# Moving the weights and activations to other places in their 256-byte period, and another order of matmuls in the first layer

## The chip, the cores and the metric

The kernel runs on one core of one Trainium2 chip. The metric is device microseconds of one execution. Before the change it takes 2504.57 us (median of 3 runs, 2503.95 to 2505.67).

## The reference

A two-layer encoder on 272 tokens (16 meta tokens and 256 tokens of input), width 2048, everything in float32. One layer is:

```
h = RMSNorm(x)
[q | k | v | f | ga | gf] = h @ W_in
a = attention(q, k, v) @ W_attn_br ; s = Re(2-D DFT of f) @ W_four
x = x + (sigmoid(ga) * a + sigmoid(gf) * s) @ W_out
x = x + W_down( silu(dwconv3(RMSNorm(x) @ W_up_gate)) * (RMSNorm(x) @ W_up_val) )
```

The meta tokens are dropped at the end. Nearly all the work is products of the activations (272 tokens wide) with weight matrices that are each read once.

## The kernel before

**Three matmuls for one product.** Activations and weights are float32. TensorE runs them in a format of shorter mantissa, so each operand is cut into a high part (a rounded copy) and a low part (what is left), and a product is made of three matmuls: high weights with high activations, high weights with low activations, low weights with high activations. Below they are called a *triple*. In the code they are lines 384, 385 and 386 in `group`, in that order. The weights are the stationary operand (a 128x128 load ahead of each matmul), the activations the moving one: 272 columns in the first layer, and in the second 258 (columns 14 to 271) but for the keys and values, which have 272.

**Chunks and groups.** Weights come in chunks of 512 rows by 256 columns: CW = 4 row blocks (`c`) by MG = 2 column blocks (`m`) of 128x128. `load_raw` (L266) brings a chunk from memory through SP's DMA queue, `split_w` makes the high part on ScalarE (L313) and the low part on VectorE (L315), four row blocks in one instruction each, two chunks ahead of the chunk in use (LOOK = 2). `group` runs all chunks of one pair of output blocks: `ps[0]` and `ps[1]` are two accumulators in PSUM, and a chunk has 4 x 2 = 8 triples, 24 matmuls. In all chunks but a group's last the order is c = 0, m = 0; c = 0, m = 1; c = 1, m = 0 and so on, so that two triples in a row read the same activations. In a group's last chunk it is c = 0 to 3 for m = 0, and then c = 0 to 3 for m = 1, so that the first accumulator is done half a chunk early. This is the sort at L370 and L371. After each second triple `step()` and `pump()` hand out other work (norms, rotary, splits), whatever the order.

**Which groups there are.** The first layer has groups of 4 chunks (f 2 and 3, k, v, four q, eight ga, eight gf, 22 ug, 22 uv), of 2 chunks (eight a, sixteen o), of 6 (eight d) and of 5 (eight d): 108 groups, 408 chunks, of which 300 are not the last of their group. Two more f groups are run by `first_groups`, which has an order of its own, and the s groups by `four_group`. In the second layer `group` runs k, v, q, ga, gf, a, o and ug, 224 chunks, and the uv groups that are left (L380, L381); the rest of that layer, `ps_p` and `ps_t`, has the activations stationary and 512 columns of weights moving (L1474, L1555).

**Where the operands lie.** A row of activations is 272 x 4 = 1088 bytes, 4 x 256 + 64. A row block of a chunk is given the same 1088 bytes (CS = T), of which 1024 are used. So when `c` goes up by one, activations and weights both move by 64 bytes within a period of 256 bytes, and their distance within that period stays what it was. The distance is set by where tiles begin: the constants X_AT, G_AT, M_AT and Q_AT are numbers of float32 by which the activations are moved into their tiles (xHL; gHL; mH and mL; qH and qL), and W_PAD puts 128 bytes between the three buffers of high weights and those of low weights. LOW = 60 puts the low activations of a tile at 16 bytes less than the high ones within the period. Worked out from the sizes of the tiles in the order in which they are allocated, in bytes modulo 256, at c = 0 and the first column that a matmul uses:

| | high activations | low activations | high weights | low weights |
|---|---|---|---|---|
| before, both layers | 108 | 92 | 128 | 0 |
| before, keys and values of layer 2 | 52 | 36 | 128 | 0 |
| before, split activations of `ps_p` (`opnd`, stationary) | 128 | 128 | 128 | 0 |

The order of the instructions on TensorE is that of the program. There is no wait in `group` other than those for the split weights, for the activations and for a free PSUM bank.

Of the kernel before, what the change touches and what calls it, by code (L numbers as in the profile page):

```python
# [10 lines left out]
F32 = mybir.dt.float32  # L11
F32R = mybir.dt.float32r
# [4 lines left out]
P = 128  # L17
# [15 lines left out]
CW = 4  # L33
# [28 lines left out]
F0 = 1536  # L62
CS = T
LOW = 60
X_PAD, X_AT = 192, (59, 45)
G_AT, G_PAD = 43, 128
M_AT, M_PAD = ((27, 23), (5, 1)), (60, 22)
Q_AT, Q_PAD = (((43,), (47,)), ((45, 29), (41, 41))), (((76,), (84,)), ((62, 46), (62, 62)))
W_PAD = 32
A_PAD, O_AT = 48, 16  # L70

def _branch(text):
# [91 lines left out]
def encoder_kernel(ctx, tc, xT, params, consts, bmat, cfold, csign, w_fl, w_f64c, w_in, w_abr, w_four, w_f64, w_out, w_up, w_down, w_vn, w_dn, w_dt, out):  # L164
    nc = tc.nc
    per = ctx.enter_context(tc.tile_pool(name="per", bufs=1))
    wp = ctx.enter_context(tc.tile_pool(name="wp", bufs=3))
# [10 lines left out]
    for l in range(DEPTH):  # L178
        def g(w, mg, k0, k1):
            return [(w[l, mg, c], CW) for c in range(k0 // CW, k1 // CW)]  # L180
# [11 lines left out]
        for half in range(2):  # L192
            for kind, j in BRANCH_ORDER[half]:
                w, off, n = {"ga": (w_in, IN_GA, KT), "gf": (w_in, IN_GF, KT), "s": (w_four, 0, 8), "a": (w_abr, 0, 8)}[kind]
                chs = [(fw[KT + 2 * j + c], CW) for c in range(2)] if (l, kind) == (1, "s") else g(w, off + j, 0, n)
# [23 lines left out]
    chunks, folded, streamed, mix, summed, stage, small_w = [], set(), set(), {}, {}, {}, {}  # L219
    t, done = 0, 0  # L220
# [25 lines left out]
    raws, splits = {}, {}  # L246
# [24 lines left out]
    def advance(upto):  # L271
        while st["raw"] < min(upto + RAW + extra(upto), len(chunks)):
            load_raw(st["raw"])
            st["raw"] += 1
        while st["fetch"] < min(upto, len(chunks)):
            i = st["fetch"]
            if i in folded:
                todo.append((i, lambda i=i: fold_w(i)))
            for a in (0, 2) if i <= 3 else (0,):
                todo.append((i, lambda i=i, a=a: split_w(i, a, a + 2 if i <= 3 else CW)))  # L280
            st["fetch"] += 1

    def pump(upto=None):
        if upto is None:
            if todo:
                todo.pop(0)[1]()
        while upto is not None and todo and todo[0][0] <= upto:
            todo.pop(0)[1]()
# [7 lines left out]
    def weight_rows(w, dense):  # L296
        if dense:
            return w[:, :CW * MG * P].rearrange("p (c m) -> p c m", c=CW)
        return w.rearrange("p (c m) -> p c m", c=CW)[:, :, :MG * P]

    def split_w(i, a, b, parts="hl"):
        if i not in splits:
            new = []
            for t in ("wh", "wl"):
                new.append(weight_rows(wp.tile([P, CW * CS], F32R, tag=t, name=f"{t}{i}"), i in streamed))
                if i == 0:
                    wp.tile([P, W_PAD], F32, tag=t + "_pad", name=t + "_pad", bufs=1)
            splits[i] = tuple(new)
        h, lo = splits[i]
        st["wl"] = lo  # L310
        r = raws[i]
        if "h" in parts:
            nc.scalar.copy(h[:, a:b], r[:, a:b])  # L313
        if "l" in parts:
            nc.vector.tensor_tensor(lo[:, a:b], r[:, a:b], h[:, a:b].bitcast(F32), op=ALU.subtract)  # L315
            if b == CW:
                del raws[i]
# [8 lines left out]
    def step(force=False):  # L326
        if not force and slow[1] and slow[2]:
            slow[0] -= 1
            if slow[0] <= 0:
                slow[0] = slow[2]  # L330
                if next(slow[1], None) is None:
                    slow[1] = None
        for s in shadow:
            s[0] -= 1
        for s in list(shadow):
            if force or s[0] <= 0:
                try:
                    s[0] = next(s[1])
                except StopIteration:
                    shadow.remove(s)  # L340
                return
# [9 lines left out]
    def next_split():  # L351
        i = st["next"]
        advance(i + 1 + LOOK)
        pump(i)
        st["next"] += 1
        return splits.pop(i)

    def group(key, rhs, width, tag="mm"):
        k, chs = order[st["grp"]]
        assert k == key, (k, key)  # L360
        st["grp"] += 1
        nm = "_".join(str(v) for v in key)
        ps = [psum.tile([P, 512], F32, tag=tag, name=f"ps_{nm}_{m}") for m in range(MG)]
        nk = CW * len(chs)
        for j in range(len(chs)):
            for _ in range(mix.get((key, j), 0)):
                next(st["products"])
            h, lo = next_split()
            cm = [(c, m) for c in range(CW) for m in range(MG)]
            if j == len(chs) - 1:  # L370
                cm.sort(key=lambda v: v[1])  # L371
            for n, (c, m) in enumerate(cm):
                kt = CW * j + c
                x = rhs(kt)
                sl = slice(m * P, (m + 1) * P)
                o = ps[m][:, :width]
                if len(x) == 1:
                    ab = x[0]
                    o2 = ps[m][:, :2 * width].rearrange("p (r n) -> p r n", r=2)
                    nc.tensor.matmul(o2, h[:, c, sl], ab, start=kt == 0, stop=False)  # L380
                    nc.tensor.matmul(o, lo[:, c, sl], ab[:, 0, :], start=False, stop=kt == nk - 1)  # L381
                else:
                    a, b = x
                    nc.tensor.matmul(o, h[:, c, sl], a, start=kt == 0, stop=False)  # L384
                    nc.tensor.matmul(o, h[:, c, sl], b, start=False, stop=False)  # L385
                    nc.tensor.matmul(o, lo[:, c, sl], a, start=False, stop=kt == nk - 1)  # L386
                if n % 2:
                    step()
                    pump()
        return ps  # L390
# [36 lines left out]
    def first_groups(pss):  # L427
# [4 lines left out]
        for kt in range(KT // CW * 2 * CW):  # L432
            q, j, c = kt // (2 * CW), kt // CW % 2, kt % CW
            k = CW * q + c
            if c == 0:
                if kt == 0:
                    norm_split(0, P_NM)
                    split_w(0, 0, 1)
                    norm_split(1, P_NM)
                    split_w(0, 1, 2)  # L440
                    norm_split(2, P_NM)
                    split_w(0, 2, 4)
                    norm_split(3, P_NM)
                    st["fetch"] = 1
                h, lo = splits.pop(st["next"])
                st["next"] += 1
# [194 lines left out]
    for l in range(DEPTH):  # L641
# [7 lines left out]
        with tc.tile_pool(name=f"mix{l}", bufs=1) as mp:  # L649
# [105 lines left out]
            if l == 0:  # L755
# [19 lines left out]
                with tc.manual_schedule(engines={mybir.EngineType.PE, mybir.EngineType.DVE}):  # L775
                    ps = group((l, "f", 2), xr(0), T, "aux")
# [7 lines left out]
                tc.keep_in_program_order(nc.vector.tensor_tensor(br3[64:96], brem[32:64], br3[32:64].bitcast(F32), op=ALU.subtract))  # L784
                tc.keep_in_program_order(nc.vector.tensor_scalar(bgh, prm[:, P_BG:P_BG + DEPTH * 2 * KT], 0.5, None, op0=ALU.mult))
                f_evac(3, group((l, "f", 3), xr(0), T))
            else:
                push(norm_stats(hold), 8)
# [188 lines left out]
            VL = mp.tile([P, NKV, 2, P], F32R, name="VL")  # L977

            ps = group((l, "k", 0), xr(0), T)
            until(hold, "tok2")  # L980
            tok, tok2 = hold["tok"], hold["tok2"]
# [220 lines left out]
            for i in range(4):  # L1202
# [3 lines left out]
                if last:  # L1206
                    if i in (0, 2):
                        until(hold, "vt" if i == 0 else "fold")
                        for t_, n in ((qH, "q1"), (qL, "q2")):
                            o = Q_AT[l][t_ is qL][i // 2]  # L1210
                            t = mp.tile([P, 4 * T + Q_PAD[l][t_ is qL][i // 2]], F32R, tag=n + "ab"[i // 2], name=n)
                            t_.append(t[:, o:o + 4 * T].rearrange("p (h t) -> p h t", t=T))
                elif i == 0:
                    until(hold, "vt")
                    until(hold, "fold")
                    for t_, n in ((qH, "q1"), (qL, "q2")):
                        o = Q_AT[l][t_ is qL][0]
                        t = mp.tile([P, NH * T + Q_PAD[l][t_ is qL][0]], F32R, tag=n, name=n)[:, o:o + NH * T].rearrange("p (h t) -> p h t", t=T)
# [26 lines left out]
            for half in range(2):  # L1245
                mH = mL = None
                for n_, (kind, i) in enumerate(BRANCH_ORDER[half]):
                    if half or last and n_ >= 4:
                        slow[2] = 22
                    j = i - 4 * half  # L1250
# [42 lines left out]
        with tc.tile_pool(name=f"ffn{l}", bufs=1) as fp:  # L1293
# [32 lines left out]
            for c, n in enumerate(() if last else FF_SPLIT):  # L1326
                gf = fp.tile([P, FF_SPLIT[0] * 2 * T + G_PAD], F32R, tag="gHL", name="gHL")
                gH, gL = (gf[:, G_AT + (FF_SPLIT[0] * T + LOW) * r:G_AT + (FF_SPLIT[0] * T + LOW) * r + FF_SPLIT[0] * T].rearrange("p (k t) -> p k t", t=T) for r in range(2))
                for i in range(k0 // MG, (k0 + n) // MG):
                    cs = conv_gate(i)  # L1330
                    ps = group((l, "uv", i), xr(0), T)
                    for m in range(MG):
                        j = 2 * i + m - k0
# [10 lines left out]
            if last:  # L1344
# [152 lines left out]
                for i in UP_ORDER:  # L1497
# [16 lines left out]
                    for m in range(0 if i in VPAIRS else MG):  # L1514
                        j = 2 * i + m
# [21 lines left out]
                for b in TAIL_ORDER:  # L1537
                    k, chs = order[st["grp"]]
# [5 lines left out]
                    for j in range(len(chs)):  # L1544
                        for _ in range(mix.get((k, j), 0)):
                            next(st["products"])
                        wh, wl = (w.rearrange("p (k a) m -> p k (a m)", k=2) for w in next_split())
# [86 lines left out]
```

## Time and profile before

| | |
|---|---|
| median of the runs | 2504.57 us |
| the profiled execution's own time | 2504.27 us |
| its span, first to last instruction | 2502.3 us |
| TensorE busy | 2493.7 us (100%), 18848 matmuls |
| weight loads busy | 2411.3 us (96%) |
| VectorE, ScalarE, GpSimd busy | 1987.5, 1338.4, 204.8 us |
| DMA | 706.85 MB, 282 GB/s |

Matmuls are pipelined, and the ends that the profile gives are modelled: a matmul of 272 columns is shown with some 283 ns, while the next one starts some 123 ns after it. So what a stretch of matmuls costs is read from starts: the start of the first matmul of the next stretch less that of its own first.

### The profile page before, as it was taken

How to read it: one execution, taken by the hardware profiler on the slowest of the kernel's cores; microseconds unless marked ns; L12 is line 12 of the kernel's file. 1: busy time of each engine (PE TensorE's matmuls, PEld its weight loads, DVE VectorE, ACT ScalarE, POOL GpSimd, SP SyncE). 2: the span in 40 equal slices, each digit the busy share in tenths (PEclk: the TensorE clock that was granted, in tenths of full speed). 3: DMA queues.
4: the chain of work that ended last, by engine and by line, in shares of the span. 5: the costliest groups of instructions: out<-in, count | busy, mean ns of one | idle time of the engine just before them, and what ended most of it. 6: DMA issues, size and time to landing. Idle time of an engine off the chain costs nothing.

```text
span 2502.3 us, 47930 instructions
## 1 busy us (share of the span) xinstructions
PE 2493.7 (100%) x18848; PEld 2411.3 (96%) x18848; DVE 1987.5 (79%) x3155; ACT 1338.4 (53%) x1913; POOL 204.8 (8%) x394
## 2 busy tenths in 40 slices
PE   9999999999999999999999999999999999999999
PEld 9999999999999999999999999999988899988887
DVE  7787866778878667888778887666878787898898
ACT  6455534454444334444445565444676665666665
POOL 0000000012212222222210000000000000000000
PEclk9999999999999999999999999999999999999999
DMA  7544557879989999999985647888878886788887
GB/s 250 170 156 163 189 195 250 261 259 373 400 323 381 402 389 373 397 380 391 391 294 199 197 151 246 267 262 273 252 268 293 296 291 237 260 282 293 283 298 267
DMA packets 194802, 706.85 MB, mean 282 GB/s; under 512 B 22144, under 2 KB 27392, under 8 KB 194320
## 3 DMA queue, kind: packets, MB, share of 16 engines
q1 hardware_dynamic: 146768, 517.09, 58.1%
q0 software_dynamic: 46368, 184.57, 21.3%
q8 instruction: 147, 2.41, 0.4%
q10 hardware_dynamic: 1440, 2.13, 0.2%
q14 instruction: 79, 0.65, 0.1%
HBM read 623.32 MB, written 111.15 MB: 294 GB/s over the span
## 4 chain that ended last, share of the span: by engine, by line
PE 100%; DMA 0%; DVE 0%; ACT 0%; SPq 0%; issue 0%
PE ps_p L1474 14%; PE ps_ug L386 7%; PE ps_ug L384 7%; PE ps_ug L385 7%; PE ps_d L386 3%; PE ps_uv L386 3%; PE ps_uv L384 3%; PE ps_d L384 3%; PE ps_uv L385 3%; PE ps_d L385 3%; PE ps_o L385 2%; PE ps_ga L385 2%; PE ps_ga L386 2%; PE ps_gf L384 2%; PE ps_gf L385 2%; PE ps_ga L384 2%
## 5 line engine op out<-in xcount | busy, mean ns | idle before, releaser
L315 DVE TENSOR_TENSOR wl<-raw,wh 128x1024 fp32r<-128x1024 f32 (+1 forms) x961 | 1158.7, 1217 | 397.8 <-ACT wh L313 388.2
L313 ACT CAST wh<-raw 128x1024 fp32r<-128x1024 f32 (+1 forms) x961 | 996.8, 1042 | 888.1 <-PE ps_ug L385 201.7
L384 PE MATMUL ps_ug<-xHL,wh 128*128 128x272 f32 (+1 forms) x1408 | 398.6, 283 | 0.0
L386 PE MATMUL ps_ug<-xHL,wl 128*128 128x272 f32 (+1 forms) x1408 | 397.0, 283 | 0.0
L385 PE MATMUL ps_ug<-xHL,wh 128*128 128x272 f32 (+1 forms) x1408 | 396.8, 282 | 0.0
L385 PEld LDWEIGHTS ps_ug<-xHL,wh 128*128 128x128 f32 x1408 | 265.5, 189 | 3.3
L384 PEld LDWEIGHTS ps_ug<-xHL,wh 128*128 128x128 f32 x1408 | 263.9, 187 | 3.6
L386 PEld LDWEIGHTS ps_ug<-xHL,wl 128*128 128x128 f32 x1408 | 263.4, 188 | 0.9 <-DVE wl L315 0.4
L1474 PE MATMUL ps_p<-wh,opnd 128*128 128x512 f32 x816 | 222.9, 393 | 0.0
L384 PE MATMUL ps_uv<-xHL,wh 128*128 128x272 f32 x704 | 201.1, 286 | 0.0
L384 PE MATMUL ps_d<-gHL,wh 128*128 128x272 f32 x704 | 201.1, 286 | 0.0
L386 PE MATMUL ps_d<-gHL,wl 128*128 128x272 f32 x704 | 201.0, 285 | 0.0
L386 PE MATMUL ps_uv<-xHL,wl 128*128 128x272 f32 x704 | 200.9, 285 | 0.0
L385 PE MATMUL ps_uv<-xHL,wh 128*128 128x272 f32 x704 | 199.8, 284 | 0.0
L385 PE MATMUL ps_d<-gHL,wh 128*128 128x272 f32 x704 | 199.7, 284 | 0.0
L1474 PEld LDWEIGHTS ps_p<-wh,opnd 128*128 128x128 f32 x816 | 148.3, 188 | 29.7 <-ACT wh L313 0.2
L547 DVE TENSOR_TENSOR wi<-wi,wi 128x512 f32<-128x512 f32 x224 | 147.0, 684 | 0.1
L384 PE MATMUL ps_ga<-xHL,wh 128*128 128x272 f32 (+1 forms) x512 | 146.7, 287 | 0.0
L384 PE MATMUL ps_gf<-xHL,wh 128*128 128x272 f32 (+1 forms) x512 | 145.7, 285 | 0.0
L385 PE MATMUL ps_o<-mL,wh 128*128 128x272 f32 (+1 forms) x512 | 144.8, 283 | 0.0
L384 PE MATMUL ps_o<-mH,wh 128*128 128x272 f32 (+1 forms) x512 | 144.6, 282 | 0.0
L386 PE MATMUL ps_ga<-xHL,wl 128*128 128x272 f32 (+1 forms) x512 | 144.6, 282 | 0.0
(381 smaller groups left out, 5952.4 us busy)
## 6 DMA issues: line engine op xcount, KB each, us to landing
raw<-in_w_up SPq DMA_DIRECT2D x288, 512.0 KB, 6.3
raw<-in_w_in SPq DMA_DIRECT2D x191, 512.0 KB, 4.0
raw<-in_w_down SPq DMA_DIRECT2D x88, 512.0 KB, 7.0
wi<-in_w_dn POOLq DMA_DIRECT2D x80, 512.0 KB, 9.2
ft<-wi POOLq DMA_DIRECT2D x80, 512.0 KB, 7.3
raw<-ft SPq DMA_DIRECT2D x80, 512.0 KB, 4.7
raw<-in_w_out SPq DMA_DIRECT2D x64, 512.0 KB, 4.3
raw<-fv SPq DMA_DIRECT2D x64, 512.0 KB, 4.5
```

Of the source, the lines that this page charges most:

```text
L313: nc.scalar.copy(h[:, a:b], r[:, a:b])
L315: nc.vector.tensor_tensor(lo[:, a:b], r[:, a:b], h[:, a:b].bitcast(F32), op=ALU.subtract)
L384: nc.tensor.matmul(o, h[:, c, sl], a, start=kt == 0, stop=False)
L385: nc.tensor.matmul(o, h[:, c, sl], b, start=False, stop=False)
L386: nc.tensor.matmul(o, lo[:, c, sl], a, start=False, stop=kt == nk - 1)
L547: tt = lambda *v, **kw: tc.keep_in_program_order(nc.vector.tensor_tensor(*v, **kw))
L1474: nc.tensor.matmul(ps[h], x, w[:, 512 * h:512 * h + 512], start=fresh and (s_, q) in BEGIN and first, stop=(s_, q) in END and end, skip_gr ...
```

## The change

The weights' padding goes, so that high and low weights both begin at 128 within the period, and all the activations are moved by 64 bytes up (X_AT of the first layer by 48 float32 down, which is the same within the period):

| | high activations | low activations | high weights | low weights |
|---|---|---|---|---|
| after, both layers | 172 | 156 | 128 | 128 |
| after, keys and values of layer 2 | 116 | 100 | 128 | 128 |
| after, `opnd` | 128 | 128 | 128 | 128 |

If the period is cut into four lines of 64 bytes, both weights then lie in the line of the activations, where before the high weights lay in the line behind theirs (higher) and the low weights in the line before (lower). The place of an activation within its 64 bytes (44 for the high, 28 for the low) is the same before and after.

And in the first layer every chunk of a group, not the last alone, is run in the order of m: four row blocks into the first accumulator, then four into the second.

```diff
-X_PAD, X_AT = 192, (59, 45)
-G_AT, G_PAD = 43, 128
-M_AT, M_PAD = ((27, 23), (5, 1)), (60, 22)
-Q_AT, Q_PAD = (((43,), (47,)), ((45, 29), (41, 41))), (((76,), (84,)), ((62, 46), (62, 62)))
-W_PAD = 32
+X_PAD, X_AT = 192, (11, 61)
+G_AT, G_PAD = 59, 128
+M_AT, M_PAD = ((43, 39), (21, 17)), (60, 22)
+Q_AT, Q_PAD = (((59,), (63,)), ((61, 45), (57, 57))), (((76,), (84,)), ((62, 46), (62, 62)))
...
     def split_w(i, a, b, parts="hl"):
         if i not in splits:
-            new = []
-            for t in ("wh", "wl"):
-                new.append(weight_rows(wp.tile([P, CW * CS], F32R, tag=t, name=f"{t}{i}"), i in streamed))
-                if i == 0:
-                    wp.tile([P, W_PAD], F32, tag=t + "_pad", name=t + "_pad", bufs=1)
-            splits[i] = tuple(new)
+            splits[i] = tuple(weight_rows(wp.tile([P, CW * CS], F32R, tag=t, name=f"{t}{i}"), i in streamed) for t in ("wh", "wl"))
...
             cm = [(c, m) for c in range(CW) for m in range(MG)]
-            if j == len(chs) - 1:
+            if key[0] == 0 or j == len(chs) - 1:
                 cm.sort(key=lambda v: v[1])
```

No instruction is added or taken away: the pads were memory alone.

## The prediction

> **What bounds the kernel now.** I began with the page's span, its shares and its chain of waits.
>
> ```profile
> span 2502.3 us, 47930 instructions
> PE 2493.7 (100%) x18848; PEld 2411.3 (96%) x18848; DVE 1987.5 (79%) x3155; ACT 1338.4 (53%) x1913; POOL 204.8 (8%) x394
> ...
> PEclk9999999999999999999999999999999999999999
> ...
> PE 100%; DMA 0%; DVE 0%; ACT 0%; SPq 0%; issue 0%
> ```
>
> The matmuls alone set the end: TensorE is busy all the time at the full granted clock, and the chain holds nothing else. The view of TensorE's waits confirms it; this is all of it:
>
> ```profile
> PE ps_f L451 <- ACT wh L313: 4.7, 2, 4.5
> PE ps_uv L381 <- DVE wl L315: 0.3, 1, 0.3
> ```
>
> So the change matters only through the pace of the matmuls, and the question is whether their pace depends on their order and addresses at all. That is read from the timeline, from starts. First the o groups of the first layer, which have two chunks, one in the alternating order and then one in the order of m (start, duration, instruction):
>
> ```profile
> 477.39 0.28 PE L384 MATMUL ps_o<-mH,wh 128*128 128x272 f32 x1
> 480.35 0.29 PE L384 MATMUL ps_o<-mH,wh 128*128 128x272 f32 x1
> 483.34 0.28 PE L384 MATMUL ps_o<-mH,wh 128*128 128x272 f32 x1
> ...
> 525.02 0.28 PE L384 MATMUL ps_ug<-xHL,wh 128*128 128x272 f32 x1
> ```
>
> The alternating chunk takes 480.35 - 477.39 = 2.96 us, the sorted one 2.99, for the same 24 matmuls. Eight such groups take 525.02 - 477.39 = 47.63, 5.954 each. The d groups have six chunks, and the first and last of eight of them are:
>
> ```profile
> 811.08 0.28 PE L384 MATMUL ps_d<-gHL,wh 128*128 128x272 f32 x1
> 825.90 0.29 PE L384 MATMUL ps_d<-gHL,wh 128*128 128x272 f32 x1
> 828.90 0.28 PE L384 MATMUL ps_d<-gHL,wh 128*128 128x272 f32 x1
> ...
> 953.64 0.28 PE L384 MATMUL ps_ug<-xHL,wh 128*128 128x272 f32 x1
> ```
>
> Five alternating chunks take 14.82 us, the sorted sixth 3.00 (two decimals, so it is 2.99 to 3.01 here). A group's first chunk takes the 2.96 of the o groups, and the other four then (14.82 - 2.96) / 4 = 2.965. Eight groups take 142.56, 17.82 each, and 17.82 - 14.82 = 3.00 again. For a sorted chunk I use 5.954 - 2.96 = 2.994, and 2.992 to stay between it and the row's 2.99.
>
> The prices of a triple follow. A sorted chunk is eight at 2.992 / 8 = 0.374. In an alternating pair the first triple moves on to new activations, as each sorted one does, and the second reads the same ones again; if the first costs 0.374, the second costs 2.965 / 4 - 0.374 = 0.367. Call these the slow and the fast price; 0.007 us, 2%, lies between them. The split of a pair into these two is inferred; the sums are read.
>
> **The change part by part.** Nothing is added or removed on any queue: no instruction, no DMA, no semaphore. SP's loads and the splits are handed out at the same places, since `step()` and `pump()` follow the count of triples and not their order.
>
> *The order of m in 300 more chunks of the first layer.* Each goes from 2.965 to 2.992, 0.027 us more. A group's first chunk starts from 2.96 and keeps what makes it start quicker (its first triple, where the activations jump back), so it too pays 0.027. The sum is 300 x 0.027 = +8.1 us, all on the path, since there is nothing beside TensorE in the chain. With the weights' and activations' old places this is near to read off, for the program ran both orders in 408 chunks.
>
> Could the new order wait? It wants all four row blocks of the split weights in the first half of a chunk, not over the whole of it. One instruction of VectorE makes all four:
>
> ```profile
> 850.83 1.23 DVE L315 TENSOR_TENSOR wl<-raw,wh 128x1024 fp32r<-128x1024 f32 x1 [0.53 <-ACT wh L313]
> ...
> 855.61 0.29 PE L384 MATMUL ps_d<-gHL,wh 128*128 128x272 f32 x1
> ```
>
> It ends at 852.06, and with two chunks ahead it serves the chunk that starts at 855.61: 3.5 us to spare, where either order reads the first row block at the very start. So I cost it at nothing; the cover is those 3.5 us of chunks already split. If it were gone, the cost would be a split's 1.23 us for each late chunk. The buffer of a chunk is free after its last matmul in both orders, and a group's last chunk, after which the accumulators are read, was sorted already.
>
> *The new places.* The pads cost no time, and their 256 bytes move all later tiles by a whole period. What changes is the distance from activations to weights: high to high from -20 to +44 bytes, low activations to low weights from +92 to +28, both modulo 256, and the next triple's weights, loaded while the third matmul runs, from -84 (or -20 within an alternating pair) to -20 in the sorted order. No row shows the first two distances with 272 columns, so the cost is bounded from both sides.
>
> The nearest row in kind is that of the products of the second layer, where moving high weights lie in the line of the stationary activations (128 and 128) and moving low weights two lines off (0 and 128):
>
> ```profile
> 2285.61 1.08 PE L1474 MATMUL ps_p<-wh,opnd 128*128 128x512 f32 x4
> 2286.53 0.62 PE L1474 MATMUL ps_p<-wl,opnd 128*128 128x512 f32 x2
> 2287.00 0.28 PE L384 MATMUL ps_ug<-xHL,wh 128*128 128x258 f32 x1
> ...
> 2291.66 1.08 PE L1474 MATMUL ps_p<-wh,opnd 128*128 128x512 f32 x4
> 2292.59 0.62 PE L1474 MATMUL ps_p<-wl,opnd 128*128 128x512 f32 x2
> 2293.04 0.39 PE L1474 MATMUL ps_p<-wh,opnd 128*128 128x512 f32 x1
> ```
>
> In the same line a matmul takes 0.92 / 4 = 0.230 and 0.93 / 4 = 0.2325 us, two lines off 0.47 / 2 = 0.235 and 0.45 / 2 = 0.225: 0.231 against 0.230 on the mean. There the line makes no difference that adds up. I take this value, zero, for the places, as it is the one row pair that has weights and activations in one line and in two with all else equal.
>
> The upper end comes from the keys of the second layer, whose high and low activations (52 and 36) do lie in the line of the low weights (0), though also 8 bytes further on within a line:
>
> ```profile
> 1310.20 0.29 PE L384 MATMUL ps_k<-xHL,wh 128*128 128x272 f32 x1
> ...
> 1313.26 0.29 PE L384 MATMUL ps_k<-xHL,wh 128*128 128x272 f32 x1
> ```
>
> That is 3.06 us for an alternating first chunk of 272 columns, 0.10 over the first layer's 2.96. On 408 chunks it is +41 us, in place of the order's +8. The lower end is the fast price for every triple: 8 x 0.367 = 2.936 a chunk. In the first layer that saves 300 x 0.029 = 8.7 us and, in the 108 last chunks, 108 x 0.056 = 6.0. In the second layer, whose order stays:
>
> ```profile
> 1599.69 0.28 PE L384 MATMUL ps_o<-mH,wh 128*128 128x258 f32 x1
> 1602.49 0.28 PE L384 MATMUL ps_o<-mH,wh 128*128 128x258 f32 x1
> 1605.33 0.28 PE L384 MATMUL ps_o<-mH,wh 128*128 128x258 f32 x1
> ```
>
> its alternating chunk takes 2.80 and its sorted one 2.84, so by the same split slow is 0.355 and fast 0.345, and a chunk of fast triples 2.76: some 0.04 saved in each of 216 chunks, 9 us (an estimate). Together -24 us.
>
> **The sum** is made against the profiled execution's own 2504.27 us: +8.1 for the order, 0 for the places, **2512.4 us**. That execution is 0.30 us under the median of the runs, 2504.57, so nothing is to be corrected. Its span of 2502.3 leaves 2.0 us around it that the change doesn't touch.
>
> **The rivals.**
>
> *All triples at the fast price (faster).* What makes a triple slow may be the load of the next weights two lines off while new activations come in. At present a fast triple follows a third matmul whose next weights lie at -20, and a slow one follows one at -84. After the change the sorted order has -20 there throughout. If that distance decides, and the others don't, the first layer saves 8.7 + 6.0 = 14.7 us: 2489.6, with the second layer down to 2480. For it speaks that the two prices go with this distance in every alternating pair; against it, that a group's first triple, after a jump of the activations, is quick at -84 as well, and that 384 and 385 get new distances too. It decides from the place of the weights on: the order with the old places would still cost.
>
> *Weights in the activations' line are slow.* The price of the layer-2 keys in the first layer: 2504.3 + 41 = 2545. Against it stands the pair of products, and that those keys start elsewhere within a line.
>
> *A group's last chunk is slow because it is last.* Then the order is worth nothing, nor are the places, and the time stays at 2504.3. For it: last and sorted go together in every group shown. Against it: a sorted chunk is slow evenly, in triples far from the group's end, and nothing of the group's end is in these matmuls.
>
> *The places do nothing by rule.* The Trainium skill, TensorE: Matmul & The Clock Gate, section Step-by-step: what each phase is for, says that TensorE reads moving and stationary operands through two independent ports, so that loading the next weights takes no bandwidth from the running matmul. By it neither distance nor order has a price, and the time would be 2504.3, the last rival's. The 2.96 against 2.99 above already goes against it as far as the order is concerned; for the places no row here decides.
>
> **How the numbers follow.** The forecast (order costs, places nothing) gets 0.41, the fast price 0.23, the slow line 0.15, no change 0.21. A difference under 0.2%, 5.0 us, is about what a measurement of this kernel can't tell from none, so same is 2499.6 to 2509.6. The forecast's own range is 2507 to 2518 (the order at 0.025 to 0.030 a chunk, the places at 2 us either way and some more), of which a tenth lies under 2509.6: slower 0.37 + 0.15 = 0.52, and some 0.03 from the slow side of no change; same 0.04 + 0.18 = 0.22; faster 0.23. The range for 8 in 10 reaches from 2486, a third of the way from the first layer's fast price (2489.6) to that of both layers (2480), to 2526, a little over half of the slow line's cost.
>
> **What would show it.** Right: TensorE's busy share and its chain at 100% as before; chunks of the first layer's d and o groups all at 2.99, the six of a d group 17.95 in place of 17.82; o groups of the second layer at 2.80 and 2.84 still; no new wait of TensorE for `wh` or `wl`. The fast price shows as 2.94 a chunk in the first layer, the slow line as 3.06, no change as 2.965 in all but the last. I am wrong on the order if, with the new places, a sorted chunk of the first layer takes 2.965 or less; and wrong on the places if the second layer's chunks, where the order stays, move by more than 0.02.

## The result, and the profile after

The changed kernel takes 2485.3 us (median of 4 runs, 2484.46 to 2485.95), the kernel before, beside it on the same chip, 2505.12 (4 runs, 2503.95 to 2505.72). The ratio is 0.9921, with a 95% interval of 0.9904 to 0.9938: faster by 19.8 us, 0.8%. I had forecast 2512.4, slower by 8.

The page's head and its chain of waits, after:

```profile
span 2483.2 us, 47930 instructions
...
PE 2474.7 (100%) x18848; PEld 2393.2 (96%) x18848; DVE 1987.1 (80%) x3155; ACT 1339.4 (54%) x1913; POOL 203.7 (8%) x394
...
PEclk9999999999999999999999999999999999999999
...
PE 100%; DMA 0%; DVE 0%; ACT 0%; SPq 0%; issue 0%
```

All that TensorE waits for, after (engine, line of the stalled matmul, what released it: us in total, times, longest):

```profile
PE ps_f L445 <- ACT wh L307: 4.6, 2, 4.4
PE ps_uv L375 <- DVE wl L309: 0.3, 1, 0.3
```

The same number of matmuls, the same clock, a chain of TensorE alone, and the same two waits. The span is 19.1 us shorter only because matmuls follow each other more closely. Line numbers are six lower than before: the triple is now L378, L379 and L380.

The timeline after, by starts (start, duration, instruction): the first d group of the first layer and the one behind it, the end of eight such groups, and the first key of layer 2:

```profile
805.85 0.29 PE L378 MATMUL ps_d<-gHL,wh 128*128 128x272 f32 x1
...
820.59 0.29 PE L378 MATMUL ps_d<-gHL,wh 128*128 128x272 f32 x1
...
823.53 0.29 PE L378 MATMUL ps_d<-gHL,wh 128*128 128x272 f32 x1
...
947.29 0.29 PE L378 MATMUL ps_ug<-xHL,wh 128*128 128x272 f32 x1
...
1300.89 0.29 PE L378 MATMUL ps_k<-xHL,wh 128*128 128x272 f32 x1
```

Eight d groups of six chunks take 947.29 - 805.85 = 141.44 us, or 141.44 / 48 = 2.947 a chunk, the first five (14.74) and the sixth (2.94) alike. Before, it was 142.56, with 2.965 for an alternating chunk on the mean and 2.99 for a sorted one. Every chunk of the first layer is sorted now, and those of the d groups are all faster than either kind was before. The first key of layer 2 starts at 1300.89 in place of 1310.20, so the first layer gives 9.3 us.

In the second layer, where the order stayed, eight o groups after:

```profile
1587.78 0.28 PE L378 MATMUL ps_o<-mH,wh 128*128 128x258 f32 x1
...
1590.56 0.28 PE L378 MATMUL ps_o<-mH,wh 128*128 128x258 f32 x1
...
1593.34 0.28 PE L378 MATMUL ps_o<-mH,wh 128*128 128x258 f32 x1
...
1632.31 0.29 PE L412 MATMUL ps_s<-fr,wh 128*128 128x276 f32 x1
```

The alternating chunk goes from 2.80 to 2.78 and the sorted one from 2.84 to 2.78. Sixteen chunks take 44.53 us, 2.783 each. So the second layer, which has only the new places, is faster as well: with 19.1 us in the span and 9.3 in the first layer, some 9.8 are its share, that of its products (`ps_p`, `ps_t`) included.

### The profile page after: what moved, and what is told of

Same layout as the page of the kernel before. It is cut to its first block, busy times and chain, and to the rows that moved or that the text cites. A ratio compares the mean times of both kernels' runs of the same rounds, so it can differ in the third digit from the quotient of the medians.

```text
span 2483.2 us, 47930 instructions
## 1 busy us (share of the span) xinstructions
PE 2474.7 (100%) x18848; PEld 2393.2 (96%) x18848; DVE 1987.1 (80%) x3155; ACT 1339.4 (54%) x1913; POOL 203.7 (8%) x394
## 4 chain that ended last, share of the span: by engine, by line
PE 100%; DMA 0%; DVE 0%; ACT 0%; SPq 0%; issue 0%
PE ps_p L1468 14%; PE ps_ug L378 7%; PE ps_ug L380 7%; PE ps_ug L379 7%; PE ps_uv L378 4%; PE ps_d L378 4%; PE ps_uv L380 3%; PE ps_d L380 3%; PE ps_d L379 3%; PE ps_uv L379 3%; PE ps_gf L378 3%; PE ps_ga L378 2%; PE ps_o L378 2%; PE ps_ga L380 2%; PE ps_gf L380 2%; PE ps_o L380 2%
## 5 line engine op out<-in xcount | busy, mean ns | idle before, releaser
L378 PE MATMUL ps_ug<-xHL,wh 128*128 128x272 f32 (+1 forms) x1408 | 397.8, 283 | 0.0
L379 PE MATMUL ps_ug<-xHL,wh 128*128 128x272 f32 (+1 forms) x1408 | 394.4, 280 | 0.0
L380 PE MATMUL ps_ug<-xHL,wl 128*128 128x272 f32 (+1 forms) x1408 | 394.1, 281 | 0.0
L379 PEld LDWEIGHTS ps_ug<-xHL,wh 128*128 128x128 f32 x1408 | 264.8, 188 | 3.2
L378 PEld LDWEIGHTS ps_ug<-xHL,wh 128*128 128x128 f32 x1408 | 264.3, 188 | 3.3
L380 PEld LDWEIGHTS ps_ug<-xHL,wl 128*128 128x128 f32 x1408 | 263.6, 188 | 1.3 <-DVE wl L309 1.0
L378 PE MATMUL ps_uv<-xHL,wh 128*128 128x272 f32 x704 | 201.3, 286 | 0.0
L378 PE MATMUL ps_d<-gHL,wh 128*128 128x272 f32 x704 | 201.3, 286 | 0.0
L379 PE MATMUL ps_uv<-xHL,wh 128*128 128x272 f32 x704 | 199.2, 283 | 0.0
L379 PE MATMUL ps_d<-gHL,wh 128*128 128x272 f32 x704 | 199.2, 283 | 0.0
L380 PE MATMUL ps_d<-gHL,wl 128*128 128x272 f32 x704 | 198.9, 283 | 0.0
L380 PE MATMUL ps_uv<-xHL,wl 128*128 128x272 f32 x704 | 198.9, 283 | 0.0
L378 PE MATMUL ps_ga<-xHL,wh 128*128 128x272 f32 (+1 forms) x512 | 146.5, 286 | 0.0
L378 PE MATMUL ps_gf<-xHL,wh 128*128 128x272 f32 (+1 forms) x512 | 145.4, 284 | 0.0
L378 PE MATMUL ps_o<-mH,wh 128*128 128x272 f32 (+1 forms) x512 | 144.1, 282 | 0.0
L379 PE MATMUL ps_ga<-xHL,wh 128*128 128x272 f32 (+1 forms) x512 | 143.6, 280 | 0.0
L380 PE MATMUL ps_ga<-xHL,wl 128*128 128x272 f32 (+1 forms) x512 | 143.5, 280 | 0.0
```

## The experiments

In all of them the distance is that of activations to weights modulo 256 bytes, as in the table of the change: after it, +44 for the high activations, +28 for the low ones against both weights; the weights loaded during a triple's third matmul, those of the next triple, stand at -20. Every kernel has the same 18848 matmuls, and the granted clock is 1.0 in all of them. Ratios and differences are to the kernel before, run beside each. Most runs show the eight d groups of the first layer, 48 chunks, by the first matmul of theirs and the first one behind them; the time of a chunk is the difference over 48. The two that sort only some chunks, or sort at the old places, show the first d group and the start of the next.

**One edit at a time: the order alone.** The kernel before, with

```diff
-            if j == len(chs) - 1:
+            if key[0] == 0 or j == len(chs) - 1:
```

> The kernel before, with the order of m in all chunks of the first layer and the old places. My sum and the next-weights theory: each of 300 chunks goes from 2.965 to 2.992 us, 2505.1 + 8.1 = 2513.2. The theory that a last chunk is slow because it is last: chunks stay at 2.965, 2505. The line theory, if the order has no price of its own but with the weights away from the line: as my sum.

Measured: 2512.4 us against 2504.73 for the kernel before, ratio 1.003 (1.0019 to 1.0042): +7.7. The timeline of this kernel:

```profile
815.07 0.28 PE L384 MATMUL ps_d<-gHL,wh 128*128 128x272 f32 x1
...
830.03 0.29 PE L384 MATMUL ps_d<-gHL,wh 128*128 128x272 f32 x1
...
833.02 0.28 PE L384 MATMUL ps_d<-gHL,wh 128*128 128x272 f32 x1
```

Five chunks take 14.96, 2.992 each, and the sixth 2.99. The order's price at the old places is what the kernel before showed, and the 8.1 us of the sum hold. The rival that a last chunk is slow because it is last is out: all six are alike.

**The places alone.** The changed kernel with the old order:

```diff
-            if key[0] == 0 or j == len(chs) - 1:
+            if j == len(chs) - 1:
```

> The changed kernel with the old order in the first layer: only a group's last chunk is in the order of m. Line theory (what counts is that the weights lie in the activations' line; the order then has no price): the chunks stay near the 2.947 us of the changed kernel and the time near 2485. Order price as I summed it, on top of the places: an alternating chunk is 0.027 us cheaper than a sorted one, 2.92 us, 2485.3 - 8.1 = 2477. Next-weights theory (my rival: what counts is the distance of the next weights, loaded while a triple's third matmul runs; here it is -20 in one triple of a pair only): half of the gain of the first layer is lost, 2.965 us a chunk, 2485.3 + 300 x 0.018 = 2491.

Measured: 2491.34 us, ratio 0.9946 (0.9931 to 0.9961): -13.4. Its timeline:

```profile
810.06 0.29 PE L378 MATMUL ps_d<-gHL,wh 128*128 128x272 f32 x1
...
824.89 0.29 PE L378 MATMUL ps_d<-gHL,wh 128*128 128x272 f32 x1
...
827.84 0.29 PE L378 MATMUL ps_d<-gHL,wh 128*128 128x272 f32 x1
```

An alternating chunk takes 14.83 / 5 = 2.966, within 0.002 of its price at the old places (14.82 / 5); the sorted one 2.95 in place of 2.99. So in the first layer the places are worth nothing to an alternating chunk and 0.045 us to a sorted one. The two edits do not add: alone they give +7.7 and -13.4, together -19.8 and not -5.7. The 14.1 us between are the 300 chunks for which both were changed: at the old places sorting costs 2.992 - 2.965 = 0.027, at the new ones it saves 2.966 - 2.947 = 0.019, and 300 x 0.046 = 13.8.

**One of the two weights in the line.** The changed kernel with pads of 128 bytes, once behind each kind of weights, which moves the low ones to 0 and leaves the high ones, and once ahead of each kind, which moves the high ones to 0 and leaves the low ones. Of the first:

```diff
...
+                new.append(weight_rows(wp.tile([P, CW * CS], F32R, tag=t, name=f"{t}{i}"), i in streamed))
+                if i == 0:
+                    wp.tile([P, W_PAD], F32, tag=t + "_pad", name=t + "_pad", bufs=1)
...
```

> The changed kernel with the pads back, so that the high weights lie in the activations' line as in the changed kernel (128 against 172) and the low weights two lines off (0). Line theory with an equal price for each matmul: the low weights are one of three, so a third of the gap between order alone (2513) and the changed kernel (2485) is lost: about 2494. Next-weights theory: the weights that follow a third matmul are high ones, whose distance stays at -20, so nothing is lost: 2485.

> The changed kernel with pads ahead of the weights, so that the low weights lie in the activations' line (128 against 172) and the high weights two lines off (0). Line theory with an equal price for each matmul: two of three matmuls lose their gain, 2485 + 2/3 x 28 = about 2504. Next-weights theory: the distance of the next weights is 128 away from -20, so all of the gain is lost: about 2513. If the low weights alone were what counts: 2485.

Measured: with the low weights away 2511.74 us, ratio 1.0028 (1.0018 to 1.0039); with the high weights away 2522.84, ratio 1.0073 (1.0058 to 1.0088). The timeline of the first, with the second layer's eight o groups:

```profile
817.88 0.29 PE L384 MATMUL ps_d<-gHL,wh 128*128 128x272 f32 x1
...
961.88 0.29 PE L384 MATMUL ps_ug<-xHL,wh 128*128 128x272 f32 x1
...
1609.45 0.28 PE L384 MATMUL ps_o<-mH,wh 128*128 128x258 f32 x1
...
1653.98 0.29 PE L418 MATMUL ps_s<-fr,wh 128*128 128x276 f32 x1
```

and of the second:

```profile
818.79 0.29 PE L384 MATMUL ps_d<-gHL,wh 128*128 128x272 f32 x1
...
962.79 0.29 PE L384 MATMUL ps_ug<-xHL,wh 128*128 128x272 f32 x1
...
1613.21 0.28 PE L384 MATMUL ps_o<-mH,wh 128*128 128x258 f32 x1
...
1658.70 0.29 PE L418 MATMUL ps_s<-fr,wh 128*128 128x276 f32 x1
```

Either way a chunk of the first layer takes 144.00 / 48 = 3.000. A third of the gain was to be lost with the low weights and two thirds with the high ones; all of it is lost with either, and some more. So no price per matmul adds up to this. It also refutes my rival as I had put it: with the low weights away, the next triple's weights are still at -20 in the sorted order, and nothing is fast. The second layer answers otherwise: its 16 chunks take 44.53 us with the low weights away, as in the changed kernel, and 45.49 with the high ones away.

**Both weights together, in another line.** The changed kernel with one pad ahead of the weights, and its rest to 256 bytes behind them, of 192, 128 or 64 bytes:

```diff
+            if i == 0:
+                wp.tile([P, W_PAD], F32, tag="w_pad", name="w_pad", bufs=1)
...
```

> The changed kernel with both weights moved together by 192 bytes, so that they still lie in one line with each other but one line of 64 bytes behind the activations (172 - 64 = +108, +92 for the low ones; the next triple's weights at +44). Line theory (the weights must lie in the activations' own line): the gain is lost, 2.99 us a chunk in the first layer. Together theory (high and low weights must share a line, wherever it is): 2.947 stays. Next-weights theory (only -20 or 236 for the next triple's weights is fast): 2.99.

> The changed kernel with both weights moved together by 128 bytes: two lines off the activations (+172, +156; the next triple's weights at +108). Line theory and next-weights theory: 2.99 us a chunk in the first layer. Together theory: 2.947.

> The changed kernel with both weights moved together by 64 bytes, one line above the activations (-20, -36; the next triple's weights at -84, as in the kernel before). Line theory and next-weights theory: 2.99 us a chunk in the first layer, the sorted chunk's price of before. Together theory: 2.947.

Measured in one run each, so no interval: 2517.61, 2521.61 and 2516.2 us, against 2504.85 for the kernel before. The timelines, in this order:

```profile
817.43 0.29 PE L383 MATMUL ps_d<-gHL,wh 128*128 128x272 f32 x1
...
961.43 0.29 PE L383 MATMUL ps_ug<-xHL,wh 128*128 128x272 f32 x1
```

```profile
818.65 0.29 PE L383 MATMUL ps_d<-gHL,wh 128*128 128x272 f32 x1
...
962.65 0.29 PE L383 MATMUL ps_ug<-xHL,wh 128*128 128x272 f32 x1
```

```profile
815.47 0.28 PE L383 MATMUL ps_d<-gHL,wh 128*128 128x272 f32 x1
...
959.10 0.28 PE L383 MATMUL ps_ug<-xHL,wh 128*128 128x272 f32 x1
```

That is 3.000, 3.000 and 2.992 a chunk. It isn't enough that high and low weights share a line: of these four lines only the activations' own is fast. The last kernel's 2.992 is the price of the order alone, though the low weights lie 128 bytes apart in these two; with the high weights at -20 the place of the low ones had no price in the first layer. In the second it had one: the sixteen o chunks take 45.60 us in this kernel and 45.17 in the one with the order alone.

**The next triple's weights.** The changed kernel with the row blocks run downward, and `start` and `stop` moved to the first and last block in this order:

```diff
-                cm.sort(key=lambda v: v[1])
+                cm.sort(key=lambda v: (v[1], -v[0]))
...
```

> The changed kernel with its places, but the row blocks of a sorted chunk run from c = 3 down to 0. Every triple keeps its own distances (+44, +28, +44); only the next triple's weights, loaded while the third matmul runs, go from -20 to +108. Line theory: 2.947 us a chunk in the first layer, 2485. Next-weights theory: 2.99 a chunk, 2485.3 + 408 x 0.046 = 2504. If a next distance of +108 is another fast one, less than 2485.

Measured: 2499.16 us, ratio 0.9976 (0.9966 to 0.9987), so 13.9 slower than the changed kernel. Its timeline:

```profile
811.71 0.28 PE L379 MATMUL ps_d<-gHL,wh 128*128 128x272 f32 x1
...
954.43 0.28 PE L379 MATMUL ps_ug<-xHL,wh 128*128 128x272 f32 x1
```

142.72 / 48 = 2.973: between the two theories. A triple's own distances are what they were, so what follows a triple does count, with 2.973 - 2.947 = 0.026 a chunk, or 408 x 0.026 = 10.6 us. The first layer bears that out: the first key of layer 2 starts at 1311.22 us in place of 1300.89. The other 3 are of the second layer, whose sorted last chunks run downward as well: its sixteen o chunks take 45.28 us in place of 44.53. I put it down to the load that runs beside the third matmul, but the activations' rows are read downward too, and no run takes the two apart. And it is about half of the 0.053 that lie between the own line and the others (3.000). So the distance of a triple's own weights has a price, and so, most likely, has that of the next ones.

"Own" needs a word. In the trace of the changed kernel a matmul's weights are loaded while the matmul before it runs: the load for an L379 starts at 809.91 us, beside the matmul of L378 that starts at 809.90. So two of a triple's three loads run beside its own matmuls, that of the low weights beside the one with the low activations (+28), and only the third is the next triple's. The runs don't tell whether the own distances count by these loads or in another way.

**The place within the line.** The changed kernel with the first layer's activations at other places, a different one for each tile; of the first kernel:

```diff
-X_PAD, X_AT = 192, (11, 61)
-G_AT, G_PAD = 59, 128
-M_AT, M_PAD = ((43, 39), (21, 17)), (60, 22)
+X_PAD, X_AT = 192, (15, 61)
+G_AT, G_PAD = 55, 128
+M_AT, M_PAD = ((41, 37), (21, 17)), (60, 22)
```

> The changed kernel with the first layer's activations moved within their line of 64 bytes, by a different amount in each tile: xHL 16 bytes up (high at +60, low at +44 from the weights), gHL 16 down (+28, +12), mH and mL 8 down (+36, +20). The line of all of them stays that of the weights, but for no part of these. If the line is all that counts: 2.947 us a chunk in ug, d and o groups alike. If the place within the line counts too, the three differ; that of the kernel before and after is +44 from a line's start, and nothing here says which other is better or worse, save that 8 bytes up from it the keys of layer 2 take 3.06.

> As the run beside it, with xHL 8 bytes up (+52, +36: the place within a line that the keys of layer 2 have), gHL 32 bytes down (+12, and the low ones at -4, so in the line above), and mL 16 bytes up (low activations at the place of the high ones, both +44). If the line is all that counts: 2.947 in ug and o groups, more in d. If the place within the line is what made the keys of layer 2 slow, ug groups take 3.06; if their slowness is of that layer, 2.947.

Measured in one run each: 2500.36 and 2521.75 us, against 2505.7. In the first kernel, o groups (16 chunks), d groups (48) and the 80 chunks of ug and uv between the two stretches of d groups:

```profile
319.31 0.29 PE L378 MATMUL ps_o<-mH,wh 128*128 128x272 f32 x1
...
368.18 0.29 PE L412 MATMUL ps_s<-fr,wh 128*128 128x276 f32 x1
...
814.39 0.29 PE L378 MATMUL ps_d<-gHL,wh 128*128 128x272 f32 x1
...
958.39 0.29 PE L378 MATMUL ps_ug<-xHL,wh 128*128 128x272 f32 x1
...
1196.25 0.29 PE L378 MATMUL ps_d<-gHL,wh 128*128 128x272 f32 x1
```

and in the second:

```profile
327.00 0.29 PE L378 MATMUL ps_o<-mH,wh 128*128 128x272 f32 x1
...
374.58 0.28 PE L412 MATMUL ps_s<-fr,wh 128*128 128x276 f32 x1
...
831.62 0.29 PE L378 MATMUL ps_d<-gHL,wh 128*128 128x272 f32 x1
...
974.34 0.29 PE L378 MATMUL ps_ug<-xHL,wh 128*128 128x272 f32 x1
...
1218.61 0.29 PE L378 MATMUL ps_d<-gHL,wh 128*128 128x272 f32 x1
```

| high, low activations from both weights | chunk of the first layer |
|---|---|
| +44, +28 (changed kernel) | 2.947 |
| +60, +44 (ug, uv) | 237.86 / 80 = 2.973 |
| +52, +36 (ug, uv) | 244.27 / 80 = 3.053 |
| +36, +20 (o) | 48.87 / 16 = 3.054 |
| +28, +12 (d) | 144.00 / 48 = 3.000 |
| +12, -4 (d) | 142.72 / 48 = 2.973 |
| +44, +44 (o) | 47.58 / 16 = 2.974 |

Eight bytes within a line cost twice what another line costs (3.053 - 2.947 = 0.106 against 0.053). Both of the slow rows have activations 4 bytes past a multiple of 16, and all the others 12 past one; no third remainder was tried. At the place of the keys of layer 2 the first layer's ug groups cost as much as those keys, though these have their high weights in another line (52 - 128 = -76). After the change the keys lie at -12 and -28, at the same place within 64 bytes, and their first chunk takes 1303.97 - 1300.89 = 3.08. So their 3.06, from which I took the upper end, looks like the price of a place within the line and not of the line. No place that was tried is better than that of the change.

**Distance or address.** Two last kernels: one pad of 32 bytes ahead of the weights and none behind, which moves the weights and gHL, mH and mL, but not xHL; and both weights with all activations of the first layer 64 bytes up. Of the first:

```diff
+            if i == 0:
+                wp.tile([P, 8], F32, tag="w_pad", name="w_pad", bufs=1)
...
```

> The changed kernel with one pad of 32 bytes ahead of the weights, which moves the weights and all tiles behind them by 32 bytes, gHL, mH and mL with them, while xHL, ahead of the weights, stays. So d and o groups keep their distances (+44, +28) and only begin elsewhere within a line of 64 bytes (weights at 32, activations at 12); ug groups keep the place of their activations (44) and get the distances +12 and -4. Relative theory (only distances count): d and o stay at 2.947 us a chunk, ug goes to 2.973, what d groups showed at +12 and -4. Absolute theory (where an activation lies within its 64 bytes counts): d and o go to 2.973, ug stays at 2.947.

> The changed kernel with both weights and all activations of the first layer moved up together by 64 bytes: the same distances and the same places within 64 bytes, in another line of the period. If the period of 256 bytes has no line of its own that counts, the first layer stays at 2.947 us a chunk; if the line itself counts, it moves. The second layer's activations stay, so its weights go to -20 and -36, one line above them, and its o chunks should show what the run with both weights 64 bytes up showed: 2.85 us.

Measured in one run each: 2499.9 and 2499.59 us, against 2504.02. The first kernel's d groups and the ug and uv behind them, then the second's d groups:

```profile
811.12 0.28 PE L380 MATMUL ps_d<-gHL,wh 128*128 128x272 f32 x1
...
952.56 0.29 PE L380 MATMUL ps_ug<-xHL,wh 128*128 128x272 f32 x1
...
1190.43 0.28 PE L380 MATMUL ps_d<-gHL,wh 128*128 128x272 f32 x1
```

```profile
805.82 0.29 PE L383 MATMUL ps_d<-gHL,wh 128*128 128x272 f32 x1
...
947.26 0.29 PE L383 MATMUL ps_ug<-xHL,wh 128*128 128x272 f32 x1
```

In the first, d takes 141.44 / 48 = 2.947 with the distances kept and the addresses moved, and ug 237.87 / 80 = 2.973 with the addresses of its activations kept and the distances +12, -4, which is the price that d had at +12, -4. In the second, d keeps 141.44 / 48 = 2.947, and o of layer 2, one line away from its weights, goes to 2.85 (its 16 chunks run from 1592.21 to 1637.81 us). Only the distance counts, in these three readings of the first layer to the last digit; and 2.85 is what I had expected for one line off in the second.

## Why the prediction was wrong

**The bound: right.** TensorE is at 100% in the chain of waits of both kernels, no wait came in, and every gain or loss above is the pace of matmuls: all that TensorE waits for comes to 4.9 to 6.1 us in every kernel.

**The order of m: right at the old places, of the wrong sign at the new ones.** The run with the order alone gave +7.7 against a forecast of +8.1. But I added the two edits' prices as if they didn't depend on each other. At the new places sorting saves 0.019 us a chunk. By the mark I had set (a sorted chunk of 2.965 or less), this is wrong.

**The new places at zero: the step that failed.** The second layer's chunks, where nothing but the places changed, moved from 2.80 (alternating) and 2.84 (sorted) to 2.78 and 2.78; the mark was 0.02, and the sorted ones pass it by far. In the terms of the sum, the places put at 0 were worth -13.4 us alone, and at the new places the order's +8.1 became about -6 (19.8 - 13.4 = 6.4; 300 x 0.019 = 5.7). The zero came from one pair of products, 0.231 against 0.230 us, read off rows of two to four matmuls with two decimals. A step of 0.01 us over two to four matmuls is 0.0025 to 0.005, 1 to 2% of 0.23, and the effect looked for was 2%: the reading was no finer than its object. The profile's groups of matmuls have 1224 of these over the whole span (total busy us, mean ns). First the kernel before, with high weights in the line of the activations and low ones two lines off:

```profile
L1474 PE MATMUL ps_p<-wh,opnd 128*128 128x512 f32 x816 | 222.9, 393 | 0.0
...
L1474 PE MATMUL ps_p<-wl,opnd 128*128 128x512 f32 x408 | 126.8, 392 | 0.0
```

then the changed kernel, both in the line:

```profile
L1468 PE MATMUL ps_p<-wh,opnd 128*128 128x512 f32 x816 | 222.2, 393 | 0.0
...
L1468 PE MATMUL ps_p<-wl,opnd 128*128 128x512 f32 x408 | 126.2, 390 | 0.0
```

then the kernel with both weights two lines off:

```profile
L1473 PE MATMUL ps_p<-wh,opnd 128*128 128x512 f32 x816 | 224.9, 396 | 0.0
...
L1473 PE MATMUL ps_p<-wl,opnd 128*128 128x512 f32 x408 | 127.6, 394 | 0.0
```

Both in the line against both off is 348.4 against 352.5 us of busy time, 1.2%. The products do react to the place, which the pair I chose could not have shown; but not by lines, for with both weights one line above the activations (the run of 2516.2 us) they take 221.9 + 126.8 = 348.7 us, as in the line, and one line below 225.0 + 128.2 = 353.2. A finer reading would not have been enough, though. The change itself gave these products 349.7 - 348.4 = 1.3 us, 0.4%, and a sorted chunk of the first layer 1.5%. They have the weights moving, the activations stationary, and 512 columns: no run shows that a price of theirs holds for triples, and here it didn't.

**The lower end: near in size, its mechanism half right.** All triples at the fast price gave 2.936 a chunk in the first layer and 2.76 in the second, 2480; measured are 2.947, 2.78 and 2485.3. The first layer gave 9.3 us where this rival had 14.7, the rest 9.8 where it had 9. So the case to which I gave 0.23 is the one that came, and the time fell just under the range because I cut that case a third of its way in. Its reason was that the next weights' distance decides and the others do not. The downward order speaks for the next weights (0.026 a chunk), and the kernel with the low weights away, where they stay at -20 and a chunk takes 3.000, shows that the own distances count at least as much (0.053). That these were at a fast place too after the change was no part of it: in that its number came near by luck. With the places alone it met its mark (2.965 a chunk and 2491 expected, 2.966 and 2491.3 measured), so that run spoke for it and only the others told it from a rule of the triple's own distances.

**The other rivals.** The activations' own line is not slow: at +44, +28 it is the fastest place of all that were tried. The slowness of the keys of layer 2 goes with a place within the line, as the places within the line show. That a last chunk is slow because it is last fell with the order alone. The rule of the Trainium skill, TensorE: Matmul & The Clock Gate, section Step-by-step: what each phase is for, that the loads take no bandwidth from the running matmul, would have given the first layer one price; the runs here give 2.947 to 3.054 for the same 24 matmuls, by nothing but the distance of operands and the order, and go against it as a statement on time.

**The splits: right.** No wait for `wh` or `wl` came in with the new order.

## What to carry to other kernels

When TensorE is the bound, measure where the streamed operand lies against the stationary ones: here 24 matmuls of the same shapes and order took 2.947 to 3.054 us by the distance modulo 256 bytes alone, and 8 bytes decided more than a change of order. Don't add the prices of a new order and of new places that were each read at the other's old value: alone they were +7.7 and -13.4 us, together -19.8. And before an effect of 2% is put at zero, look whether the rows it is read from can resolve 2%; a group of a thousand matmuls can where a row of four can't. Look as well whether they are of the same kind: the products here moved by 0.4% and the sorted chunks by 1.5.

## What I had not expected

In what was tried only the distance counts and not the address: at equal distances the chunk is 2.947 us with the weights at 128 as at 192, and with all of it moved by half a line. The price has steps rather than a slope: exactly 3.000 us a chunk, 0.125 a matmul, for five different placements, and 3.053 and 3.054 for the two slowest. And it isn't the same in the two layers: in the first, with 272 columns, the low weights two lines off cost 0.053 us a chunk beside the high ones in the line, in the second, with 258, nothing (44.53 us for sixteen o chunks in both). No run changed the number of columns alone.

What makes a distance fast stays open. The runs show that the own weights' distance counts, that the line of 64 bytes and the place within it both count, and that no sum of one price for each matmul's own distance explains it: once the low weights are two lines off, moving the high ones there too costs nothing more (3.000 and 3.000), while moving the high ones alone costs 0.053. For the next weights' distance they speak without settling it. They don't show whether any reads collide, or which.
